# A mixture-of-experts block: first-layer weights loaded 2 MB at a time, 16 KB per partition, into places for pairs of slots

## The chip, the cores and the metric

The kernel runs on one core of a Trainium2 chip. The metric is the device time of one execution in microseconds (us); the time before is the median of three runs. All arithmetic on the path is float32 or float32 split into two parts; the output must agree with the reference.

## The reference

One decoder block on 256 tokens of 1024 channels, cut to what matters here (adaLN vectors `sh`, `sc`, `ga` come from the conditioning vector `c`):

```python
h = rmsnorm(x, g_mix) * (1 + sc1) + sh1
p = h @ w_in                                   # 1024 -> 8192
merged = sigmoid(p[GC]) * conformer_conv(p[CA], p[CB]) + sigmoid(p[GH]) * hgrn2(p[Q], p[F], p[I], p[G])
x = x + ga1 * (merged @ w_out)
h2 = rmsnorm(x, g_ffn) * (1 + sc2) + sh2
# mixture of experts: 32 experts, the best 4 for each token
u = h2[tokens of e] @ w1[e] + b1[e]            # 1024 -> 2048
y = clamped_swiglu(u) @ w2[e] + b2[e]          # 1024 -> 1024
x = x + ga2 * (sum of y over a token's experts, weighted)
return rmsnorm(x, g_final)
```

Each expert has 8 MB of `w1` and 4 MB of `w2` (MB here is 1024 KB), so the 32 experts bring 384 MB to the core, each byte once.

## The kernel before, in words

The program has two stages. The **mix stage** computes everything up to the router: the adaLN vectors, the product with `w_in` in blocks of 256 columns (each loaded, split in a high and a low part by ACT and by DVE or POOL, and multiplied on PE), the convolution on DVE, the recurrence, and the products with `w_ho`, `w_co` and `w_wo`. Then the **expert loop** takes experts e = 0 to 31 in order. For each it has 64 places for tokens; `gather` (line 953) picks the tokens' columns from `x2` by a matmul with a 0/1 matrix `o`, the first layer (lines 1000 and 1007) multiplies with eight row blocks `kt` of `w1`, activation and a transpose follow, and the second layer (line 1046) multiplies with four chunks of `w2`. Results are added back to the tokens two experts at a time. From e = 3 on an expert with more than 64 tokens has a second, smaller pass behind a branch (lines 1089 to 1127 and 1143 to 1157); in this input one expert takes it, e = 25. For that pass the loop holds an expert's weights until its first or second layer is over; for e = 0 to 2 every block is released as soon as it is used.

**Loads.** All weights pass through one list, `pending`, in one order, and SP's queue issues them in it (line 126). A load needs a free place; SP waits in order, so a load that waits for its place holds back all behind it. There are eight completion counters, so a load also waits until the one eight places ahead of it has landed. Before, the places are one pool, `big`, of 22 slots of 8 KB per partition, for loads and for working tiles alike. In the mix stage the table `LOADS` says after which release how many loads are issued; in the expert loop every release (`free`) issues as many as there is room for (`pump`). `w1` comes as eight loads of 1 MB (`kt`: 128 rows, one row of 8 KB per partition), `w2` as four of 1 MB (two rows of 4 KB, side by side, per partition). The tile `x2` keeps one slot in the expert loop, 21 are left for weights, which is 12 for one expert and 9 for the next.

PE and SP keep the program's order in the expert loop. In the rows of the order below, `w_w_1_3` of 128x2048 is a 1 MB load, of 128x4096 a 2 MB load; the name has the expert and the piece, and `w1` and `w2` share the name: the order in the list tells them apart.

Of the kernel before, what the change touches and what calls it, by code (L numbers as in the profile page):

```python
# [17 lines left out]
P = 128  # L18
# [15 lines left out]
NSLOT = 22  # L34
# [7 lines left out]
LOADS = (19, 0, 0, 0, 0, 0, 1, 0, 0, 1, 0, 0, 0, 0, 1, 2, 2, 2, 2, 0, 0, 1, 0, 0, 1, 1, 0, 0, 1, 0, 0, 1, 1, 0, 0, 1, 0, 0, 0, 0, 0, 0, 0, 0, 0, 1, 0, 0, 0, 1, 1, 0, 0, 0, 0, 0, 0, 1, 1, 0, 0, 1, 1, 0, 0, 1, 0, 0, 0, 0, 0, 0, 1, 0, 0, 1, 1, 0, 0, 1, 0, 0, 0, 0, 0, 1, 0, 0, 1, 1, 0, 0, 1, 1, 2, 0, 0, 0, 0, 3, 1, 0, 0, 1, 1, 0, 0, 1, 1, 3, 0, 0, 0, 0, 0, 0, 0, 0, 0, 1, 1, 1, 0, 1, 1, 2, 0, 0, 1, 0, 0, 1, 0, 0, 1, 0, 0, 1, 1, 0, 0, 0, 0, 0, 1, 1, 0, 0, 0, 0, 1, 1, 2, 1, 0, 0, 1, 0, 0, 1, 0)  # L42
# [48 lines left out]
def block_kernel(ctx, tc, xT_d, x_d, prm_d, con_d, wada0_d, wada_d, bada_d, gfin_d, win_d, wco_d, who_d, wo_d,  # L91
# [28 lines left out]
    def load():  # L120
# [3 lines left out]
        t = into if into is not None else slot(shape, "w_" + "_".join(map(str, key)), parts[0][1].dtype)  # L124
# [135 lines left out]
    ss = column_total(column_parts(xsq, "ss"), "ss")  # L260
    free()
# [20 lines left out]
    hx = [split_slot(f"h{i}") for i in range(2)]  # L282

    def mod_first(kt):
# [6 lines left out]
        free()  # L291
# [72 lines left out]
    def split_half(n, i):  # L364
# [4 lines left out]
        if i == 0:  # L369
            parts[key] = [fetch(key)]  # L370
# [1100 lines left out]
```

## Time and profile before

| | us |
|---|---|
| median of 3 runs (1325.0 to 1326.93) | 1326.85 |
| the profiled execution's own time | 1329.73 |
| its span in the trace | 1328.1 |
| PE busy | 1219.3 (92%) |
| DMA moved | 480 MB, 361 GB/s over the span |
| expert loop, first matmul of e = 0 to the end | 393.35 to 1328.1 |

PE is TensorE's matmul stream, PEld its weight loads, DVE VectorE, ACT ScalarE, POOL GpSimd, SP the engine that issues the loads. DMA share is the mean busy share of the 16 DMA engines, and packets are what one engine moves at a time. In the profile's own counts MB and GB are powers of ten: a load of 1024 KB is 1.049 MB there. The profiled execution is 2.9 us slower than the median, and sums on its trace are differences that apply to both.

### The profile page before, as it was taken

What the parts mean: (1) busy time and instruction counts of PE and PEld (TensorE: products, weight loads), DVE (VectorE), ACT (ScalarE), POOL (GpSimd) and SP (SyncE); (2) the same over time, 40 slices, a digit from 0 to 9 for tenths busy, and PEclk for the clock granted to TensorE, in tenths of its full rate; (3) what the DMA queues carried; (4) which work ended last, traced back from release to release, by engine and by line L of the source; (5) the groups of instructions that cost most, each with busy time, mean ns of one, the idle gap of its engine ahead of it and who ended that gap; (6) DMA issues with size and microseconds to landing.
All of it is one profiled execution on the core that took longest, in us unless ns stands there. A gap on an engine that the chain in (4) does not pass through costs nothing. (4 is left out here: it accounts for less than half of the span.)

```text
span 1328.1 us, 18971 instructions
## 1 busy us (share of the span) xinstructions
PE 1219.3 (92%) x7725; PEld 658.5 (50%) x7725; DVE 562.7 (42%) x1148; ACT 276.3 (21%) x439; POOL 146.3 (11%) x64
## 2 busy tenths in 40 slices
PE   5999999999899999999998998988888988999997
PEld 3899777679874443443333443333333332434432
DVE  4498999644853333332332233132322232323322
ACT  4445434654340001000010010001000000100112
POOL 3257435213300000000000000000000000000000
PEclk9999989999999999999999999999999999999999
DMA  9993336637669999999999999999999999999995
GB/s 381 409 401 119 138 128 220 222 105 291 252 271 393 421 421 419 421 420 420 421 419 421 420 420 420 421 421 419 420 420 419 419 420 420 421 409 420 420 419 213
DMA packets 71398, 480.01 MB, mean 361 GB/s; under 512 B 7521, under 2 KB 8801, under 8 KB 15970
## 3 DMA queue, kind: packets, MB, share of 16 engines
q1 hardware_dynamic: 70834, 477.47, 88.1%
q8 instruction: 91, 1.49, 0.5%
q10 hardware_dynamic: 432, 0.72, 0.2%
q14 instruction: 41, 0.34, 0.1%
HBM read 477.11 MB, written 1.05 MB: 360 GB/s over the span
## 5 line engine op out<-in xcount | busy, mean ns | idle before, releaser
L1007 PE MATMUL u_gl<-w_w,xg 128*64 128x512 f32 x1024 | 274.6, 599 | 27.8 <-DMA w_w<-in_w_dram 26.5
L1007 PE MATMUL u_lin<-w_w,xg 128*64 128x512 f32 x1024 | 271.7, 594 | 0.0
L1046 PE MATMUL yp<-w_w,li 128*64 128x512 f32 x992 | 223.0, 599 | 11.9 <-ACT li L1033 10.5
L1014 DVE TENSOR_SCALAR gl<-u_gl 128x512 f32<-128x512 f32 (+1 forms) x33 | 22.3, 675 | 334.7 <-PE u_gl L1007 326.4
L1007 PEld LDWEIGHTS u_gl<-w_w,xg 128*64 128x64 f32 x1024 | 76.6, 137 | 171.7 <-issue 87.7
L1007 PEld LDWEIGHTS u_lin<-w_w,xg 128*64 128x64 f32 x1024 | 81.5, 137 | 140.0 <-issue 140.0
L390 PEld LDWEIGHTS p_ps<-h,ws 128*128 128x128 f32 x1152 | 140.2, 192 | 12.5 <-issue 6.7
L390 PE MATMUL p_ps<-h,ws 128*128 128x256 f32 x1152 | 145.2, 286 | 0.0
L1046 PEld LDWEIGHTS yp<-w_w,li 128*64 128x64 f32 x992 | 69.4, 138 | 147.4 <-issue 125.3
L1056 DVE TENSOR_TENSOR yg<-yp,ga 64x512 f32<-64x512 f32 x60 | 41.3, 688 | 215.4 <-PE yp L1046 214.7
L376 POOL TENSOR_TENSOR ws<-w_in,ws 128x1024 fp32r<-128x1024 f32 x45 | 113.5, 2538 | 122.2 <-ACT ws L374 113.9
L1015 ACT ACTIVATE u_gl<-gl 128x512 f32<-128x512 f32 (+1 forms) x33 | 19.4, 589 | 430.2 <-DVE gl L1014 430.2
L1264 POOL PARTITION_BROADCAST w_gfin<-w_gfin x1 | 1.3, 1302 | 898.1 <-DMA w_w<-in_w_dram 898.1
L441 DVE SCALAR_TENSOR_TENSOR cv<-u,pre,cv 128x255 f32<-128x255 f32 (+25 forms) x240 | 95.2, 460 | 9.1 <-ACT cv L438 8.3
L953 PE MATMUL xg_ps<-o,w_x 128*128 128x128 f32 (+1 forms) x512 | 62.9, 282 | 14.1 <-DVE li L1016 10.2
L374 ACT CAST ws<-w_in 128x1024 fp32r<-128x1024 f32 x64 | 66.0, 1046 | 46.6 <-PE p_ps L390 23.6
L953 PEld LDWEIGHTS xg_ps<-o,w_x 128*128 128x128 f32 x512 | 60.1, 196 | 26.9 <-DVE li L1016 21.7
L1059 ACT ACTIVATE ys0h<-yg,by 64x512 fp32r<-64x512 f32 x30 | 21.6, 720 | 242.6 <-DVE yg L1056 242.6
L957 DVE TENSOR_SCALAR xg<-xg_ps,g,sh 128x128 f32<-128x128 f32 (+1 forms) x128 | 43.1, 401 | 18.2 <-issue 9.4
L1033 ACT COPY li<-ta 128x512 f32<-128x512 f32 (+1 forms) x33 | 18.9, 572 | 118.8 <-PE ta L1031 110.9
L376 DVE TENSOR_TENSOR ws<-w_in,ws 128x1024 fp32r<-128x1024 f32 x19 | 25.0, 1333 | 14.1 <-ACT ws L374 14.1
L390 PE MATMUL wo_ps<-ws,mg 128*128 128x256 f32 x192 | 26.2, 297 | 3.5 <-ACT ws L374 1.8
(298 smaller groups left out, 1149.0 us busy)
## 6 DMA issues: line engine op xcount, KB each, us to landing
w_w<-in_w_dram SPq DMA_DIRECT2D x380, 1024.0 KB, 19.8
w_in<-in_win_dram SPq DMA_DIRECT2D x32, 1024.0 KB, 11.0
w_ada<-in_wada_dram SPq DMA_DIRECT2D x24, 1024.0 KB, 15.9
w_ho<-in_who_dram SPq DMA_DIRECT2D x4, 1024.0 KB, 4.7
w_co<-in_wco_dram SPq DMA_DIRECT2D x4, 1024.0 KB, 5.0
w_wo<-in_wo_dram SPq DMA_DIRECT2D x4, 1024.0 KB, 9.6
w_w<-in_w_dram SPq DMA_DIRECT2D x8, 512.0 KB, 15.2
xT<-in_xT_dram SPq DMA_DIRECT2D x1, 1024.0 KB, 7.1
```

Of the source, the lines that this page charges most:

```text
L374: nc.scalar.copy(out=to[:, 0], in_=w[:, ks, :])
L376: (nc.vector if dve else nc.gpsimd).tensor_tensor(out=to[:, 1], in0=w[:, ks, :], in1=to[:, 0].bitcast(F32), op=ALU.subtract)
L390: nc.tensor.matmul(out, lhsT=lt, rhs=rh, start=first and kt == 0 and i == 0, stop=kt == KT - 1 and i == 2, skip_group_check=not first)
L441: nc.vector.scalar_tensor_tensor(out=cv[:, ct, s:], in0=u[i][:, m, :T - s], scalar=tap, in1=cv[:, ct, s:], op0=ALU.mult, op1=ALU.add)
L953: nc.tensor.matmul(ps[:, i, cs], lhsT=x2[:, t, kt * P:(kt + 1) * P], rhs=o[:, 0, t, cs], start=t == 0, stop=t == NT - 1)
L957: nc.vector.tensor_scalar(out=xg[h][:, i, cs], in0=ps[:, i, cs], scalar1=g2[:, kt:kt + 1], scalar2=sh2[:, kt:kt + 1], op0=ALU.mult, op1=AL ...
L1007: nc.tensor.matmul(up[nb][g * 64:(g + 1) * 64, :], lhsT=xg[kt // 4][:, kt % 4, i * CAP:(i + 1) * CAP], rhs=w[:, c:c + 512], start=False, s ...
L1014: nc.vector.tensor_scalar(out=gl[:, c], in0=up[0][:, c], scalar1=LIMIT, scalar2=None, op0=ALU.min)
L1015: nc.scalar.activation(si[:, c], gl[:, c], AF.Sigmoid, scale=ALPHA)
L1046: nc.tensor.matmul(yp[g * 64:(g + 1) * 64, :], lhsT=aT[:, kt % 4, kt // 4, :], rhs=w[:, kk, g * 512:(g + 1) * 512], start=False, stop=kt = ...
L1056: nc.vector.tensor_tensor(out=y[rows, :], in0=yp[gs, :], in1=ga2[gs, :], op=ALU.mult)
L1059: nc.scalar.activation(hi[rows, :], y[rows, :], AF.Copy, scale=by[rows, :])
```

## The change

`w1` is loaded as four pieces of 256 rows. Partition p holds the two neighbouring rows 2p and 2p+1 of the piece, 16 KB in one run. So the rows of `w1` that a matmul multiplies are 0, 2, 4, ... or 1, 3, 5, ... of a piece, and the token columns are picked in the same order: `gather` takes every second column of `x2` (`pick_columns`), and the scale and shift of the norm are turned once into that order (`turn_scale`, four small DMAs on ACT's queue into `by_rows`). For e = 0 the tokens were picked by `gather_rows` (matmuls of 512 columns, then four transposes); now `gather(o, half=0)` does it, 32 records of 64 columns.

The pool of 22 slots becomes 8 single slots (`big`) and 7 pairs (`two`). `w1` and most working tiles live in pairs, and `w2`, `x2` and the `w_in` blocks in singles. A piece of `w1` gives its pair back whole. The table `LOADS` is gone: after every release `pump` issues the head of the list as long as `room` finds a place of its kind; `spare` and `most_w1` limit it in the mix stage. For e = 1 the list is reordered so that the last piece of `w1` comes after the first two chunks of `w2`.

```diff
-NSLOT = 22
+NSLOT = 8
+NPAIR = 7
...
-LOADS = (19, 0, 0, 0, 0, 0, 1, 0, 0, 1, 0, 0, 0, 0, 1, 2, 2, 2, 2, 0, 0, 1, 0, 0, 1, 1, 0, 0, 1, 0, 0, 1, 1, 0, 0, 1, 0, 0, 0, 0, 0, 0, 0, 0, 0, 0, 1, 0, 0, 0, 1, 1, 0, 0, 0, 0, 0, 0, 1, 1, 0, 0, 1, 1, 0, 0, 1, 0, 0, 0, 0, 0, 0, 0, 1, 0, 0, 1, 1, 0, 0, 1, 0, 0, 0, 0, 0, 1, 0, 0, 1, 1, 0, 0, 1, 1, 2, 0, 0, 0, 0, 3, 1, 0, 0, 1, 1, 0, 0, 1, 1, 3, 0, 0, 0, 0, 0, 0, 0, 0, 0, 0, 1, 1, 1, 0, 1, 1, 2, 0, 0, 1, 0, 0, 1, 0, 0, 1, 0, 0, 1, 1, 0, 0, 0, 0, 0, 1, 1, 0, 0, 0, 0, 1, 1, 2, 1, 0, 0, 1, 0, 0, 1, 0)
...
+    two = ctx.enter_context(tc.tile_pool(name="two", bufs=NPAIR))
...
+    def pair(name, dt=F32, shape=(2 * D,)):
+
+        pairs[0] += 1
+        assert pairs[0] <= NPAIR, name
+        t = two.tile([P, 2] + list(shape), dt, tag="d", name=name)
+        return t, [t[:, i] for i in range(2)]
...
+        if key[0] == "w1":
+            pairs_w1[0] += 1
+            whole, t = pair(nm)
+            nc.sync.dma_start(out=whole.rearrange("p k f -> p (k f)"), in_=src)
+            loaded[key] = t
+            return
...
+    def room():
+        key, _, _, into = pending[0]
+        if key[0] == "w1":
+            return pairs_w1[0] < most_w1 and pairs[0] < NPAIR
+        if key[0] == "ada0":
+            return key[1] % 2 or pairs[0] < NPAIR
+        return into is not None or live[0] < NSLOT - spare
+
     def pump():
 
-        if spare is None:
-            for _ in range(next(plan, 0)):
-                load()
-        else:
-            while pending and live[0] < NSLOT - spare:
-                load()
+        while pending and room():
+            load()
...
+    def free_pair(n=1, w1=0):
+        pairs[0] -= n + w1
+        pairs_w1[0] -= w1
+        pump()
...
-        for kt in range(KT):
-            queue(("w1", e, kt), [P, 2 * FF], w1_d[e, kt * P:(kt + 1) * P, :])
+        first = len(pending)
+        for c in range(KT // 2):
+            queue(("w1", e, c), None, w1_d[e, c * 2 * P:(c + 1) * 2 * P, :].rearrange("(p k) f -> p (k f)", k=2))
...
+        if e == 1:
+
+            pending[first + 3:first + 6] = pending[first + 4:first + 6] + pending[first + 3:first + 4]
...
+    def turn_scale():
+        for h in range(2):
+            for k in range(2):
+                nc.scalar.dma_start(out=by_rows[h * 64:(h + 1) * 64, :, k::2], in_=scale2[k::2, :, h::2])
...
-                    nc.tensor.matmul(ps[:, i, cs], lhsT=x2[:, t, kt * P:(kt + 1) * P], rhs=o[:, 0, t, cs],
+                    nc.tensor.matmul(ps[:, i, cs], lhsT=pick_columns(x2[:, t, :], kt), rhs=o[:, 0, t, cs],
                                      start=t == 0, stop=t == NT - 1)
...
-    spare = 0
+    pump()
...
-    xg = gather_rows(o)
+    xg = gather(o, half=0)
...
-            return keep(w1h, ("w1", e, kt)) if inline else take(("w1", e, kt))
+            if kt % 2 == 0:
+                keep(w1h, ("w1", e, kt // 2))
+            elif not inline:
+                free_pair(0, 1)
+            return w1h[kt // 2][kt % 2]
...
-            free(KT)
+            free_pair(0, KT // 2)
```

On SP's queue, before, these are the loads that stand around the start of the expert loop: the end of e = 1 (first row the last block of its `w1`, then its four chunks of `w2`) and the beginning of e = 2. The names in brackets are what a load waits for: DMAHW is the counter of the load eight places ahead, the others are the engine that last used the place.

```order
L126 DMA w_w_1_7_4262<-in_w_dram 128x2048 [waits DMAHW7_49,PE_49]
L126 DMA w_w_1_0_4264<-in_w_dram 128x2048 [waits DMAHW0_49]
L126 DMA w_w_1_1_4266<-in_w_dram 128x2048 [waits DMAHW1_49,PE_49]
L126 DMA w_w_1_2_4272<-in_w_dram 128x2048 [waits DMAHW2_49,PE_49]
L126 DMA w_w_1_3_4278<-in_w_dram 128x2048 [waits DMAHW3_49,PE_49]
L126 DMA w_w_2_0_4284<-in_w_dram 128x2048 [waits DMAHW4_49,PE_49]
L126 DMA w_w_2_1_4290<-in_w_dram 128x2048 [waits DMAHW5_49,PE_49]
```

From the second chunk of `w2` of e = 1 on, each load waits for PE to have used one more block of e = 0. The same place of SP's queue in the changed kernel, from the third piece of `w1` of e = 1 (128x4096 is a piece of `w1`, 128x2048 a chunk of `w2`):

```order
L140 DMA w_w_1_2_4090<-in_w_dram 128x4096 [waits DMAHW4_49,DVE_49,Pool_49]
L140 DMA w_w_1_3_4210<-in_w_dram 128x4096 [waits DMAHW5_49,PE_49]
L153 DMA w_w_1_2_4212<-in_w_dram 128x2048 [waits DMAHW6_49]
L153 DMA w_w_1_3_4293<-in_w_dram 128x2048 [waits DMAHW7_49,PE_49]
L140 DMA w_w_2_0_4295<-in_w_dram 128x4096 [waits DMAHW0_49]
L140 DMA w_w_2_1_4297<-in_w_dram 128x4096 [waits DMAHW1_49]
L140 DMA w_w_2_2_4299<-in_w_dram 128x4096 [waits DMAHW2_49]
L140 DMA w_w_2_3_4348<-in_w_dram 128x4096 [waits DMAHW3_49,PE_49]
```

The fourth chunk of `w2` of e = 1 takes the eighth single, which is the place of the first chunk of `w2` of e = 0; three pieces of `w1` of e = 2, whose pairs wait for nothing more, stand behind it.

Later in SP's queue of the changed kernel, from the branch of e = 25's second pass (the row of line 1345 is the branch behind the first layer, that of line 1379 the branch behind the second):

```order
L1345 COMPARE_AND_BRANCH
L1345 UNCONDITIONAL_BRANCH x2
L140 DMA w_w_26_3_10793<-in_w_dram 128x4096 [waits DMAHW3_49,PE_49]
L153 DMA w_w_26_0_10795<-in_w_dram 128x2048 [waits DMAHW4_49]
L153 DMA w_w_26_1_10797<-in_w_dram 128x2048 [waits DMAHW5_49]
L153 DMA w_w_26_2_10799<-in_w_dram 128x2048 [waits DMAHW6_49]
L1379 COMPARE_AND_BRANCH
L1379 UNCONDITIONAL_BRANCH x2
L153 DMA w_w_26_3_10896<-in_w_dram 128x2048 [waits DMAHW7_49,PE_49]
L140 DMA w_w_27_0_10898<-in_w_dram 128x4096 [waits DMAHW0_49]
```

The last piece of an expert's `w1` waits for the first layer of the expert before, and the last chunk of its `w2` for the second layer of the expert before.

On PE, before, the start of e = 0's tokens stood as 8 rows of line 967, 4 transposes of line 973, and lines 1000 and 1007; in the changed kernel PE's queue there reads (line 1052 is the first layer, old line 1007):

```order
L1016 MATMUL xg_ps<-o,w_x 128x64
L984 LDWEIGHTS one_107
L984 MATMUL pc<-rt,one_107 128x32
L985 LDWEIGHTS one_107
L985 MATMUL pc<-rt,one_107 128x32
L1016 MATMUL xg_ps<-o,w_x 128x64 x15
L1045 LDWEIGHTS hots
L1045 MATMUL u_gl<-b_3513,hots 64x512
```

A gather of 64-column records stands where the products of 512 columns and the transposes stood.

## Rows read from the trace of the kernel before

**Rows 1.** The page, parts 1 and 2: busy time and share of PE and DVE, and for 40 equal slices of 33.2 us the busy tenths of PE and of the DMA engines, and GB/s.

```profile
PE 1219.3 (92%) x7725; PEld 658.5 (50%) x7725; DVE 562.7 (42%) x1148; ACT 276.3 (21%) x439; POOL 146.3 (11%) x64
...
PE   5999999999899999999998998988888988999997
...
DMA  9993336637669999999999999999999999999995
GB/s 381 409 401 119 138 128 220 222 105 291 252 271 393 421 421 419 421 420 420 421 419 421 420 420 420 421 421 419 420 420 419 419 420 420 421 409 420 420 419 213
```

**Rows 2.** The table by stages: stretch, its length, then for PE, PEld, DVE, ACT and POOL the busy us and the count, PE's granted clock, the DMA engines' busy share and GB/s.

```profile
33.20:100.00 66.80, 66.25 (x564) 60.49 (x557) 44.62 (x100) 28.84 (x42) 28.84 (x12) 0.99 0.99 403
100.00:233.00 133.00, 124.86 (x1727) 108.84 (x1725) 124.86 (x237) 59.88 (x98) 71.11 (x29) 0.96 0.42 152
233.00:393.40 160.40, 152.28 (x1105) 130.23 (x1105) 95.42 (x138) 78.60 (x127) 34.92 (x14) 0.97 0.61 232
...
393.40:416.10 22.70, 22.36 (x120) 10.37 (x120) 7.29 (x21) 1.19 (x2) 0.00 (x0) 1.00 0.87 349
...
440.80:700.00 259.20, 247.12 (x1210) 102.63 (x1208) 81.62 (x184) 25.07 (x38) 0.00 (x0) 0.99 1.01 420
700.00:1125.80 425.80, 376.72 (x1804) 148.01 (x1804) 123.91 (x281) 36.90 (x57) 0.00 (x0) 0.99 1.01 420
1125.80:1306.90 181.10, 172.48 (x899) 71.68 (x897) 52.06 (x116) 20.69 (x37) 1.30 (x1) 0.99 1.01 415
```

**Rows 3.** What PE's weight loads waited for (us in total, times, longest): the first row of the stretch 700 to 1130, then one row of the stretch 1160 to 1328.

```profile
PEld u_gl L1007 <- DMA w_w<-in_w_dram: 74.6, 58, 2.4
...
PEld u_gl L1007 <- DMA w_w<-in_w_dram: 2.5, 9, 0.3
```

**Rows 4.** PE's rows in order of time (start us, us, engine, line, operation, out<-in, count, idle before it): the first product of `gather_rows`; the start of e = 0's first layer, its gather and second layer; the end of e = 25's first layer and its second pass; the starts of e = 26 and e = 31; the end of e = 31's first layer.

```profile
388.50 1.04 PE L967 MATMUL rows_ps<-w_x,o 128*64 128x512 f32 x2 [0.17 <-DVE o L905]
...
393.35 1.08 PE L1007 MATMUL u_gl<-w_w,xg 128*64 128x512 f32 x4
...
406.28 1.03 PE L1007 MATMUL u_lin<-w_w,xg 128*64 128x512 f32 x4
...
409.05 3.68 PE L953 MATMUL xg_ps<-o,w_x 128*128 128x64 f32 x32
...
414.11 7.09 PE L1046 MATMUL yp<-w_w,li 128*64 128x512 f32 x32 [0.34 <-ACT li L1033]
...
1124.73 1.03 PE L1007 MATMUL u_lin<-w_w,xg 128*64 128x512 f32 x4
1125.69 1.07 PE L1089 MATMUL arm_ps<-w_x,owt 128*32 128x512 f32 x8
...
1157.20 1.99 PE L1157 MATMUL acc<-arm,owt 64*128 64x512 f32 x8 [0.83 <-DVE arm L1153]
...
1159.58 0.60 PE L1007 MATMUL u_gl<-w_w,xg 128*64 128x512 f32 x2
...
1290.93 1.05 PE L1007 MATMUL u_gl<-w_w,xg 128*64 128x512 f32 x4
...
1306.85 1.98 PE L1067 MATMUL acc<-ys,owt 64*128 64x512 f32 x4
```

**Rows 5.** SP's waits from 393 to 440 (us in total, times, longest), SP's single load at 416.09 and at 426.83 in order of time, and, for the loads at 395.3, 426.83 and 1102.96 alone, the time from issue to landing (min/median/max of one).

```profile
SPq L126 <- PE u_lin L1007: 30.5, 16, 10.4
SPq L126 <- PE yp L1046: 12.3, 4, 8.3
...
416.09 0.33 SPq L126 DMA_DIRECT2D w_w<-in_w_dram  x1
...
426.83 0.33 SPq L126 DMA_DIRECT2D w_w<-in_w_dram  x1
...
DMA to landing us min/median/max: 5.1/5.1/5.1
...
DMA to landing us min/median/max: 11.5/11.5/11.5
...
DMA to landing us min/median/max: 20.8/20.8/20.8
```

**Rows 6.** The DMA queues: packets, MB, share of 16 engines. First from 393.7 to 438.3; then from 700 to 900 (loads of 8 KB rows, with the count of packets under 512 B, which are the completion counts); then from 1304.1 to 1312.9 (loads of 2 KB rows).

```profile
q1 hardware_dynamic: 2239, 16.38, 91.0%
...
DMA packets 11526, 84.05 MB, mean 420 GB/s; under 512 B 1282, under 2 KB 1282, under 8 KB 1282
q1 hardware_dynamic: 11507, 83.77, 100.8%
q8 instruction: 15, 0.25, 0.5%
...
DMA packets 1316, 2.55 MB, mean 289 GB/s; under 512 B 80, under 2 KB 80, under 8 KB 1315
q1 hardware_dynamic: 1315, 2.53, 75.9%
```

**Rows 7.** The same view from 54.9 to 95.4, where loads of 4 KB rows and of 8 KB rows alternate.

```profile
DMA packets 3076, 16.80 MB, mean 415 GB/s; under 512 B 258, under 2 KB 258, under 8 KB 1798
q1 hardware_dynamic: 3071, 16.74, 101.2%
```

More of the change, by code (lines that the diff above doesn't have):

```diff
@@ L102, in block_kernel @@
     live = [0]
+    pairs = [0]
     pending = []
     loaded = {}
-    plan = iter(LOADS)
-    spare = None
+    spare = 1
+    pairs_w1 = [0]
+    most_w1 = 0
     def slot(shape, name, dt=F32):
@@ L123, in load @@
         parts = src if isinstance(src, list) else [(None, src)]
-        t = into if into is not None else slot(shape, "w_" + "_".join(map(str, key)), parts[0][1].dtype)
+        nm = "w_" + "_".join(map(str, key))
+        if key[0] == "w1":
[5 more added lines that the diff above has]
+        if key[0] == "ada0":
+            if key[1] % 2 == 0:
+                halves[:] = pair(nm)[1]
+            t = halves[key[1] % 2].rearrange("p (k n) -> p k n", k=KT)
+        elif into is not None:
+            t = into
+        else:
+            t = slot(shape, nm, parts[0][1].dtype)
         for at, part in parts:
@@ L281, in block_kernel @@
     s1 = of_pre(KT)
-    hx = [split_slot(f"h{i}") for i in range(2)]
+    hx = split_pair("h")
     def mod_first(kt):
@@ L290, in mod_first @@
                                  start=i == 0, stop=i == 1)
-        free()
+        if kt % 2:
+            free_pair()
         sb = temp("mod0s")
@@ L369, in split_half @@
         if i == 0:
-            parts[key] = [fetch(key)]
+            parts[key] = [fetch(key)] + split_pair("ws")
         w = parts[key][0]
-        to = split_slot("ws")
+        to = parts[key][1 + i]
         ks = slice(i * 4, i * 4 + 4)
@@ L377, in split_half @@
                                                         op=ALU.subtract)
-        parts[key].append(to)
         if i == 1:
@@ L393, in split_y @@
     def split_y(i):
[L394 removed]
+        if i == 0:
+            yx.extend(split_pair("y"))
         for kt in range(i * 4, i * 4 + 4):
@@ L411, in block_product @@
                     prod_kt(ps[:, m, :], kt, w, a, full if tokens_out else ms, ms if tokens_out else full, tokens_out, m == 0)
-            free(2 if last else 1)
+            if i == 1:
+                free_pair(2 if last else 1)
             if middle and i == 0:
@@ L600, in hgrn_out @@
         square_sums(*before)
-        free(3)
+        free_pair()
         orr = temp("orr")
@@ L617, in hgrn_out @@
                 yield
-        free(1)
+        free_pair()
     rbs = fix.tile([P, E], F32, name="rbs")
@@ L678, in block_kernel @@
         parts.pop(units[n])
-        free(2)
+        free_pair()
+    spare = 2
     free()
+    cv = slot([P, KT, T], "cv")
+    spare = 1
     order.__exit__(None, None, None)
@@ L702, in block_kernel @@
             if q is None:
-                q = slot([P, HEADS, T], "q")
+                q, k = (x.rearrange("p (h t) -> p h t", h=HEADS) for x in pair("qk")[1])
             nc.scalar.activation(q[:, cs, :], ps, AF.Copy, scale=float(P) ** -0.5)
@@ L732, in block_kernel @@
                 step(lv1, 100)
-                free(3)
+                free_pair()
+                free()
                 norms.append(hgrn_out())
         else:
-            if gates[i // 2] is None:
-                gates[i // 2] = slot([P, 2, KT // 2, T], "gates")
+            if gates[0] is None:
+                gates = pair("gates", F32, (2, KT // 2, T))[1]
             nc.scalar.activation(gates[i // 2][:, part - 6, i % 2 * 2:i % 2 * 2 + 2, :], ps, AF.Sigmoid)
@@ L766, in block_kernel @@
     split_y(1)
+    most_w1 = 2
     free()
@@ L781, in block_kernel @@
         nc.vector.tensor_tensor(out=lo, in0=tm, in1=hi.bitcast(F32), op=ALU.subtract)
-        if b % 2 == 1:
-            free()
+        if b == 3:
+            most_w1 = 4
+            free_pair()
         step(preps, 2)
@@ L840, in block_kernel @@
             prod_kt(ps[:, t, :], kt, w, mg, slice(0, 256), slice(t * P, (t + 1) * P), True)
-    free(4)
+    most_w1 = NPAIR
+    free_pair(2)
     residual(ps, 3, 1)
@@ L956, in gather @@
                 kt = h * 4 + i
[L957 to L976 removed]
+                nc.vector.tensor_scalar(out=xg[h][:, i, cs], in0=ps[:, i, cs], scalar1=by_rows[:, 0, kt:kt + 1],
+                                        scalar2=by_rows[:, 1, kt:kt + 1], op0=ALU.mult, op1=ALU.add)
         return xg
```

64 lines of the change are left out of this document (25 added, 39 removed).

## The prediction

> **What bounds the kernel now.** I began with the page's first parts: PE is busy for 92% of the span, but from about 395 us the DMA engines are at 9 tenths and 420 GB/s in nearly every slice [rows 1]. Two resources are near full, so I read them by stage. Up to 393.4 PE stands idle for only 0.6 + 8.1 + 8.1 = 16.8 us after the first 33 us, and DVE is busy for 124.86 of 133 us in the middle, while the loads run at 152 to 232 GB/s: the mix stage is not bound by loads [rows 2]. In the expert loop the busy share of DMA is 1.01 from 440.8 to 1125.8, and PE's falls from 247.1 of 259.2 to 376.7 of 425.8 [rows 2]. The waits say why: from 700 to 1130 PE's weight loads wait 74.6 us for loads, in 58 places, and after 1160 only 2.5 us [rows 3]. An expert's 12 loads are 12.58 MB (1.049 MB each), at 420 GB/s 29.96 us. PE without such waits needs (1290.93 − 1159.58)/5 = 26.3 us, from the start of e = 26 to that of e = 31 [rows 4]. So PE uses up its reserve, then follows the loads, until e = 25, whose second pass holds PE from 1125.69 to 1159.58 and gives the loads their lead back [rows 4]. From 1125.7 to the end PE sets the time; before that, from about e = 13, the loads do. Whatever delays the stream of loads up to the last `w1` row of e = 25 delays the end by as much; whatever shortens it is gained up to there.
>
> **The start of the loop: a gap in the loads.** Before, all 21 places are filled when e = 0 starts: 12 loads of e = 0, eight `w1` and one `w2` of e = 1. The last chunk of `w2` of e = 2, load 36, is issued at 426.83 and lands 11.5 later, at 438.3 [rows 5]. From 393.7 to there the queue moves 16.38 MB, some 15.6 loads at 369 GB/s, so it idles a little there too [rows 6].
>
> In the changed kernel the order of SP's queue sets other waits. Seven singles hold `w2`: four chunks of e = 0 and three of e = 1. The third piece of `w1` of e = 1 is in, so 20 MB have landed. The last piece waits until PE has used two row blocks: eight take 407.31 − 393.35 = 13.96, one 1.74, so 393.35 + 3.5 and 0.2 to issue = 397.1 [rows 4]. A load on an idle queue lands 5.1 after its issue [rows 5], the second MB 2.5 later (1.049/0.420): 404.7; the third chunk of `w2` 407.2. The fourth chunk takes the place of the first chunk of `w2` of e = 0, which PE uses only in its second layer, from 414.11 [rows 4]. Before, SP issued a load into that very release at 416.09 [rows 5]; the same wait now has the three pieces of e = 2 behind it, whose pairs are free. So it lands at 416.09 + 5.1 = 421.2, and the queue idles for 421.2 − 2.5 − 407.2 = 11.5 us. Then come eight MB of `w1` and four of `w2`: 12 × 2.485 − 0.33 (below) = 29.5, to 450.7 instead of 438.3. **Cost: 12.4 us of lost lead.** PE itself feels nothing at once: it needs the first of them more than 25 us later. The bounds: 9 (if the piece before lands late, the gap shrinks) and 14.
>
> **The longer rows: the gain.** From 700 to 900 the queue used 100.8% of 16 engines for 11507 − 1282 = 10225 packets of 8 KB: 3225.6/10225 = 0.3155 us each. From 1304.1 to 1312.9, with rows of 2 KB, 0.759 × 16 × 8.8/(1315 − 80) = 0.0865 us [rows 6]. The difference is 6 KB, so 2 KB cost 0.0763 and 0.0102 us is fixed in each packet. A packet of 16 KB then takes 0.6208 in place of 0.6310. A load of 1 MB has four such packets on each engine, so 0.041 us, and eight MB save **0.33 us per expert**. From e = 3 to 25 that is 23 × 0.33 = **7.6 us**. The lower bound is 0 (a row that is moved as two packets of 8 KB). The upper one comes from rows of 4 KB beside rows of 8 KB: 1.012 × 16 × 40.5 = 655.8 us, less 1273 packets of 0.3155, leaves 254.2 for 1540 packets of 4 KB, 0.165 each, so the fixed part is 0.0147 [rows 7], 0.47 per expert, 10.8 us. I take the value from the rows farthest apart, 7.6.
>
> The Trainium skill ("DMA: Bandwidth & Descriptors", "Why small descriptors are slow") puts the fixed part at some 3 cycles per packet beside 32 bytes a cycle, and calls it a matter of small descriptors. An estimate by that page is 1.5 cycles saved of 259, 0.6%, or 2.7 us in place of 7.6, and the sum would end at 1338.6. The measured step from 2 KB to 8 KB rows speaks for more than that [rows 6].
>
> **The larger piece.** PE may start a block when its load has landed. Before, one block (1.74) follows the last landing, now two: **+1.7 us**, at the end of e = 25's first layer, nowhere else on the path.
>
> **The first gather.** Before, line 967 starts at 388.50 and the first layer at 393.35; now 32 records, like those of e = 0's other half (3.68 us) [rows 4], end at 392.2, and with scaling, and 0.5 for the two products ahead, the first layer starts at 393.2 to 394.1. I take +0.3. The later gathers read every second column; they lie where PE waits for loads anyway up to e = 25. All later times hang on this start, the gap too, since a PE event ends it.
>
> **The mix stage.** PE's order there is the same; loads come earlier or later by the greedy rule, at half of the DMA rate, beside a full DVE. I take 0: the cover is DVE's 124.86 of 133. Bounds: −16.8, all of PE's idle time [rows 2], and +5.1, one load that PE waits for from its issue [rows 5]; near 0 because no stretch there has the DMA engines above 0.61. The four small DMAs on ACT come long before their first reader.
>
> **The sum.** +12.4 − 7.6 + 1.7 + 0.3 = **+6.8 us**. The load issued at 1102.96 landed at 1123.8 before the change; now the last piece lands at about 1128.9 and the layer ends near 1132.5 instead of 1125.7. The 202 us behind stay. The profiled execution becomes 1329.73 + 6.8 = 1336.5; it lies 2.9 above the median, and on the median's scale it is 1326.85 + 6.8 = **1333.7**.
>
> What is late next: with seven singles the last `w2` chunk of e = 26 waits for the end of e = 25's second pass, now 1159.1 + 6.8 = 1165.9, so it lands at 1171.0, some 3 us after its turn (1128.9 + 16 × 2.485 − 0.3 = 1168.4). The last `w1` of e = 31 comes 72 loads behind that of e = 25 (179 us): 1128.9 + 179 + 3 − 2 = 1308.9, and two blocks later 1312.4; PE arrives at 1306.85 + 6.8 = 1313.7. So PE still ends last, by about 1 us, and a smaller packet gain would make this second route the longer.
>
> **The rivals.**
> *No gain from the rows.* If 16 KB are moved at the price of two 8 KB packets, the sum is 12.4 + 1.7 + 0.3 = 14.4: 1341.3. For it: the rate is already 419 to 421 GB/s at 8 KB [rows 1]. Against it: the step from 2 KB to 8 KB [rows 6].
> *The gap is paid back: no change.* The packets save 0.51 to 0.74 per expert, so 11.7 to 17 us: about 1327. The rows of 4 KB reach 0.47, just short [rows 7]. The Trainium skill (same page, "Where 436 GB/s comes from") names a ceiling of 435.2 GB/s; rows that ran at it would take 2.409 per load and save 0.61 per expert, 14.0, which ends at 1327.2; no slice of this trace is above 421 [rows 1].
> *Faster: the loop begins earlier.* The table of loads is replaced by a rule that issues as soon as a place is free. If splits and casts got their blocks earlier, PE could regain part of its 16.8 idle us [rows 2]; it decides from 9.5 us on (6.8 + 2.7), and with 12.8 of them gone the time is 1320.9. Against it: DVE is nearly full in the middle stretch, and pairs give places back later than singles.
> *16 KB packets are slow.* The queue of instruction fetches moves packets of 16 KB (0.25 MB in 15), 0.5% of 16 × 200 us: 1.07 us each [rows 6]. At that price a `w1` of 32 packets per engine would cost 32 × 0.45 = 14 us more, 430 us over 30 experts. It is another queue, with another target, and a lone packet.
>
> **How the numbers follow.** The forecast, 0.59, own range 1330.0 to 1338.5 (gains of 10.8 to 2.7). No gain 0.16. Paid back 0.12. Earlier start 0.11. Slow packets 0.02. About 0.2%, 2.7 us, can be told from no change; the forecast's lower edge gives a little of its chance to no change, the start of the loop may help there too: faster 0.12, same 0.13, slower 0.75. The range of 1326.0 to 1341.5 leaves out the slow packets, the earlier start and half of the largest losses.
>
> **What will show it.** Right: a DMA trough of some 11.5 us at 407 to 419, SP waiting for line 1091 (the second layer) over it; packets of 16 KB near 0.62 us and 423 to 425 GB/s in the loop; PE's waits for loads beginning earlier than before, by e = 9 to 12; e = 25's first layer ending 6 to 8 us later; from there the same 202 us. Wrong: a start of the loop off 393.4 by more than 2 us; no trough; 420 GB/s as before; the end of the loop later against e = 25 than before, which would mean that the loads bind again at e = 31.

## The result and the profile after

The changed kernel took 1341.55 us (median of 6 runs, 1333.92 to 1343.02) beside 1326.70 for the kernel before, timed with it. The ratio is 1.0105, 95% interval 1.0089 to 1.0122: 13.9 us slower (11.8 to 16.2); the two medians lie 14.8 apart. The forecast was +6.8 and a range up to 1341.5. The profiled execution took 1340.79, its span is 1339.0.

The first parts of the page after, in the same form as [rows 1], and the row of the queue that carries the loads:

```profile
PE 1219.6 (91%) x7745; PEld 670.0 (50%) x7745; DVE 567.9 (42%) x1147; ACT 272.9 (20%) x438; POOL 149.2 (11%) x64
...
PE   6999799999899999999799988988888998899998
...
DMA  9865544459666999999999999999999999999995
GB/s 382 331 221 217 190 147 170 169 181 354 245 267 276 428 423 423 425 424 425 426 424 425 424 423 425 424 425 424 425 425 422 421 425 425 390 383 425 425 425 227
...
q1 hardware_dynamic: 52402, 477.46, 86.8%
```

PE is as busy as before. The loads run at 423 to 426 GB/s in the loop instead of 419 to 421, so the longer rows are faster. What is lost stands ahead of slice 14: 331 and 221 in the second and third slice where 409 and 401 stood, and 276 in the thirteenth where 393 stood. The table by stages, cut where PE's rows put the same events as in [rows 2] (the last column is GB/s, the one before it DMA's share, the one before that PE's granted clock):

```profile
33.20:100.00 66.80, 65.79 (x568) 59.89 (x568) 53.95 (x116) 32.45 (x48) 31.70 (x13) 1.00 0.76 278
100.00:233.00 133.00, 123.41 (x1717) 109.43 (x1716) 120.30 (x222) 54.33 (x91) 67.24 (x28) 0.95 0.51 183
...
396.00:418.90 22.90, 22.56 (x120) 10.48 (x118) 6.42 (x18) 1.19 (x2) 0.00 (x0) 1.00 0.47 185
418.90:443.30 24.40, 24.23 (x132) 10.91 (x128) 9.86 (x24) 2.52 (x4) 0.00 (x0) 1.00 0.95 402
443.30:700.00 256.70, 236.44 (x1144) 100.17 (x1146) 77.53 (x173) 23.75 (x37) 0.00 (x0) 0.99 1.01 425
700.00:1136.30 436.30, 386.56 (x1870) 155.20 (x1870) 129.29 (x293) 38.30 (x59) 0.00 (x0) 0.99 1.01 424
```

Where [rows 2] had a DMA share of 0.87 (393.4 to 416.1), it is now 0.47 (396.0 to 418.9). That is the trough. SP's waits from 396 to 440, its rows in order of time, and the time to landing of the two loads issued at 399.61 and at 418.85, to be read beside [rows 5]:

```profile
SPq L153 <- PE yp L1091: 18.4, 1, 18.4
...
399.61 0.33 SPq L140 DMA_DIRECT2D w_w<-in_w_dram  x1
399.99 19.18 SPq L153 DMA_DIRECT2D w_w<-in_w_dram  x2
419.23 8.96 SPq L140 DMA_DIRECT2D w_w<-in_w_dram  x4
...
w_w<-in_w_dram SPq DMA_DIRECT2D x1, 2048.0 KB, 8.6
...
w_w<-in_w_dram SPq DMA_DIRECT2D x1, 1024.0 KB, 4.9
```

SP waits 18.4 us for the second layer of e = 0 (line 1091), with three pieces of 2 MB behind the waiting load whose pairs are free; they follow from 419.23 on (the fourth of that row waits for PE). By their landings in the trace the chunk ahead of it was in at 411.3, the waiting one at 423.7, and it moved for 2.5 us itself: the queue stood idle for 423.7 − 2.5 − 411.3 = 9.9 us.

PE's rows in order of time, the same events as in [rows 4], with two of the new waits at e = 9:

```profile
395.97 1.03 PE L1052 MATMUL u_gl<-w_w,xg 128*64 128x512 f32 x4
...
416.87 7.09 PE L1091 MATMUL yp<-w_w,li 128*64 128x512 f32 x32 [0.34 <-ACT li L1078]
...
647.96 1.08 PE L1052 MATMUL u_gl<-w_w,xg 128*64 128x512 f32 x4 [1.24 <-DMA w_w<-in_w_dram]
...
652.87 1.08 PE L1052 MATMUL u_gl<-w_w,xg 128*64 128x512 f32 x4 [1.25 <-DMA w_w<-in_w_dram]
...
1136.25 1.06 PE L1134 MATMUL arm_ps<-w_x,owt 128*32 128x512 f32 x8
...
1169.44 1.03 PE L1052 MATMUL u_gl<-w_w,xg 128*64 128x512 f32 x4
...
1302.12 1.05 PE L1052 MATMUL u_gl<-w_w,xg 128*64 128x512 f32 x4
...
1318.04 1.98 PE L1112 MATMUL acc<-ys,owt 64*128 64x512 f32 x4
```

The layer of e = 25 ends 10.6 us later than in [rows 4] (1136.25 against 1125.69), and 2.6 of them were there at the start of the loop (395.97 against 393.35). The two waits are 4.91 apart, one per 2 MB piece: two blocks, then a wait. From 1136.25 to the end of the span it is 202.8 us (202.4 before).

### The profile page after: what moved, and what is told of

It is laid out like the page before. It is cut to its first block, busy times and chain, and to the rows that moved or that the text cites. A ratio compares the mean times of both kernels' runs of the same rounds, so it can differ in the third digit from the quotient of the medians.

```text
span 1339.0 us, 18731 instructions
## 1 busy us (share of the span) xinstructions
PE 1219.6 (91%) x7745; PEld 670.0 (50%) x7745; DVE 567.9 (42%) x1147; ACT 272.9 (20%) x438; POOL 149.2 (11%) x64
## 5 line engine op out<-in xcount | busy, mean ns | idle before, releaser
L1091 PE MATMUL yp<-w_w,li 128*64 128x512 f32 x992 | 223.8, 599 | 15.7 <-ACT li L1078 10.5
L1016 PE MATMUL xg_ps<-o,w_x 128*128 128x128 f32 (+1 forms) x544 | 71.0, 290 | 17.1 <-DVE li L1061 10.3
L1016 PEld LDWEIGHTS xg_ps<-o,w_x 128*128 128x128 f32 x544 | 67.6, 201 | 30.4 <-DVE li L1061 21.7
L428 ACT CAST ws<-w_in 128x1024 fp32r<-128x1024 f32 x64 | 64.1, 1048 | 13.9 <-DMA w_in<-in_win_dram 13.8
L1020 DVE TENSOR_SCALAR xg<-xg_ps,by_rows 128x128 f32<-128x128 f32 (+1 forms) x136 | 45.4, 396 | 24.8 <-PE xg_ps L1016 24.6
L430 DVE TENSOR_TENSOR ws<-w_in,ws 128x1024 fp32r<-128x1024 f32 x19 | 31.4, 1672 | 9.7 <-ACT ws L428 9.7
```

Of the source, the lines that this page charges most:

```text
L428: nc.scalar.copy(out=to[:, 0], in_=w[:, ks, :])
L430: (nc.vector if dve else nc.gpsimd).tensor_tensor(out=to[:, 1], in0=w[:, ks, :], in1=to[:, 0].bitcast(F32), op=ALU.subtract)
L1016: nc.tensor.matmul(ps[:, i, cs], lhsT=pick_columns(x2[:, t, :], kt), rhs=o[:, 0, t, cs], start=t == 0, stop=t == NT - 1)
L1020: nc.vector.tensor_scalar(out=xg[h][:, i, cs], in0=ps[:, i, cs], scalar1=by_rows[:, 0, kt:kt + 1], scalar2=by_rows[:, 1, kt:kt + 1], op0=A ...
L1091: nc.tensor.matmul(yp[g * 64:(g + 1) * 64, :], lhsT=aT[:, kt % 4, kt // 4, :], rhs=w[:, kk, g * 512:(g + 1) * 512], start=False, stop=kt = ...
```

## The experiments

Two theories went in. *Lead*: the loads start the loop late, because SP's order holds free pairs behind a chunk of `w2`, and nothing gives that lead back until e = 25. *Granularity*: places for pairs come free later and larger pieces make PE wait longer, so no order of loads helps. A third question came with the first result: what the mix stage costs, which the prediction had put at 0.

**The kernel before, once more (e0_before).**

> The kernel before, unchanged, for a second profile of it. Both theories: 1324 to 1331; the start of the expert loop within 1 us of 393.4 if the mix stage is steady; if it wanders by 2 us or more, part of the changed kernel's later start (396.0) is no property of it.

It took 1326.0, near its median, and its first layer of e = 0 starts at 390.79 instead of 393.35. So the profile the prediction used started its loop 2.6 us later than a run that is nearer to the median. Other kernels with the mix stage of before start at 389.8 and 391.7 (below). Differences of less than 2.6 us at the start, read from one profile each, mean nothing. Some profiled executions also lie above the median of their kernel: by 2.4 us in e1, 3.2 in e3 and 4.0 in e10.

**The list in the order of releases (e1_release_order).** Edit to the changed kernel, up to e = 5: each piece or chunk stands in the list where its place comes free.

```diff
+    for e in range(6):
+        early += [("w1", e + 1, 3)] * (e > 0) + [("w1", e + 2, c) for c in range(3)]
+        early += [("w2", e + 1, 3)] + [("w2", e + 2, c) for c in range(3)]
```

> The changed kernel, with the list of loads in the order in which places come free up to e = 5: after the first layer of e the last piece of w1 of e + 1 and three pieces of e + 2, after its second layer the last chunk of w2 of e + 1 and three of e + 2. Lead theory (the loads lose their lead because a load at the head of the list waits for a place of the other kind): the trough behind e = 0 goes, and so do the smaller waits up to e = 5; e = 25's first layer ends 11 to 12 us earlier than in the changed kernel (1124 to 1125 in place of 1136.3), and the time is about 1330, ratio to before 1.000 to 1.004. Rival (the lead is not what decides; the rows bring nothing, or the mix stage is what got longer): the trough goes, but the time stays within 3 us of the changed kernel's 1341.5, ratio 1.008 to 1.012.

Measured: 1329.78, ratio 1.0024 (1.0009 to 1.0038). The stages of this kernel from the start of its loop:

```profile
394.20:416.00 21.80, 21.80 (x107) 9.89 (x104) 4.66 (x13) 0.60 (x1) 0.00 (x0) 0.91 0.76 308
416.00:440.00 24.00, 23.66 (x120) 9.09 (x119) 8.32 (x21) 2.63 (x4) 0.00 (x0) 1.00 1.01 426
```

With the trough gone, at the same pieces of 2 MB, e = 25's first layer ends 730.8 us after the start of the loop (740.3 in the changed kernel, 732.3 before). Granularity falls as the main cause; lead stands. The time is still 3 us above before, although this stretch is shorter. In its profile the loop starts 0.9 us later, and what follows e = 25's first layer takes 205.5 us instead of 202.4, 2.1 of it in the second pass (36.0 us at a granted clock of 0.91; before, 33.9 at 0.95).

**The same for one expert alone (e2_one_gap).**

```diff
-    for e in range(6):
+    for e in range(1):
```

> The changed kernel, with one step of the list moved: three pieces of w1 of e = 2 come before the last chunk of w2 of e = 1. The trough of 10 to 11.5 us at e = 0 goes. If the trough itself is the cost, the time falls by 10 to 11 us, to about 1331. If the lead is bounded by the places as a whole (what is loaded earlier fills them, and the next load of the other kind waits in its turn), some 8 us of idle come back at the last chunk of w2 of e = 2, and the time falls only by 3 to 4 us, to 1338. Rival without lead: no change, 1341.5.

Measured: 1337.72, ratio 1.0081 (1.0059 to 1.0103), 3.8 less than the changed kernel. From 420 to 445 the DMA share of this kernel is 0.70: the idle time comes back one expert later, behind the last chunk of `w2` of e = 2. So it is not one slip in the list: the next last chunk waits in the same way, and with the same places only the order of e1, kept up to e = 5, takes the idle time away.

**Rows of 8 KB in pieces of 2 MB (e3_rows_8k).** The list, the places and the size of a load are those of the changed kernel; the rows are the old ones, and the turned scale is gone.

```diff
-            nc.sync.dma_start(out=whole.rearrange("p k f -> p (k f)"), in_=src)
+            nc.sync.dma_start(out=whole, in_=src)
...
-... w1_d[e, c * 2 * P:(c + 1) * 2 * P, :].rearrange("(p k) f -> p (k f)", k=2))
+... w1_d[e, c * 2 * P:(c + 1) * 2 * P, :].rearrange("(k p) f -> p k f", k=2))
```

> The changed kernel with loads of 2 MB as they are, but two rows 128 apart in each partition, 8 KB each, and the token columns picked without a stride; order, places and pieces stay. If rows of 16 KB save 0.32 us per expert, the loads take 2.485 per MB again and the end comes 7 to 8 us later than in the changed kernel, 1349, ratio to before 1.015 to 1.018. If they save nothing that reaches the end, or are paid for by the stride of the picked columns, the time stays at 1341.5, ratio 1.009 to 1.012.

Measured: 1346.19, ratio 1.0147 (1.0123 to 1.0171), a little under what was expected. The queue from 700 to 900, first in the changed kernel, then in this one (packets, MB, GB/s; then packets, MB, share of 16 engines):

```profile
DMA packets 7828, 84.86 MB, mean 424 GB/s; under 512 B 867, under 2 KB 867, under 8 KB 867
...
q1 hardware_dynamic: 7809, 84.59, 100.4%
```

```profile
DMA packets 11104, 84.08 MB, mean 420 GB/s; under 512 B 855, under 2 KB 855, under 8 KB 855
...
q1 hardware_dynamic: 11086, 83.82, 100.9%
```

The second has the rate of [rows 6] again, so the 1% belongs to the rows of 16 KB and not to the size of the load. Counted from each loop's start, e = 25's first layer ends 747.2 − 740.3 = 6.9 us later without them, 0.30 per expert over 23.

**Fewer places in the kernel before, two tries (e5_before_less, e7_before_hold).** If lost lead costs what it delays, then four slots less up to e = 11 must hurt the kernel before too.

```diff
-        spare = 3 if e == RELOAD_AFTER else 0
+        spare = 3 if e == RELOAD_AFTER else 4 if e < 12 else 0
```

> The kernel before, with four of its 22 slots kept empty in the expert loop up to e = 11, then all in use again. No load is larger or in another order. If lost lead is paid one for one, four loads of 2.485 us less in store make e = 25's first layer end 9.9 us later (about 1133 to 1136), and the time is 1336, ratio 1.0065 to 1.0085. If lead is made good later by the loads (the rival to the lead theory), the time stays within 3 us of before, ratio under 1.0023.

Measured: 1325.70, ratio 0.9996 (0.9983 to 1.0009), a miss, and no test: the DMA share from 416 to 440 is 0.98, so the loads had lost nothing. A limit on what the program counts only moved the instructions that issue; the places were there. In e7_before_hold four slots are therefore taken by tiles that small DMAs read at e = 31 (extra work of no use to the output):

```diff
+        if len(idle_places) < 4:
+            live[0] -= 1
+            idle_places.append(slot([P, 2048], f"idle{len(idle_places)}"))
```

> The kernel before, with four of its 22 slots taken out of use for good: the first four that e = 0's first layer releases get a tile that is held to the end. (The run before this one kept four free only in the program's count; the loads still got their places in time, so no load waited longer.) Lead theory: the loads wait at e = 0 until its fifth block is used, then for its second layer, and at e = 3 once more; some 8 to 11 us of idle at the start of the loop, e = 25's first layer ends 8 to 11 us later than 1122 to 1126, and the time is 1334 to 1337, ratio 1.006 to 1.0085. If lead is made good later (rival), under 1.0023.

Measured: 1338.71, ratio 1.0096 (1.0080 to 1.0112). The same event as in [rows 4], after the last block of e = 25:

```profile
1134.30 1.06 PE L1089 MATMUL arm_ps<-w_x,owt 128*32 128x512 f32 x8
```

It comes 742.6 after that loop's start (391.68), 10.3 later than before. Its 80th load of expert weights lands 165.6 after the start, before 155.7, so 9.9 of lead were lost: lead is worth its full length up to e = 25 in 1 MB loads as well, with nothing of the change in the kernel. The time is above what was expected because the loads bind once more at e = 31.

**One chunk earlier still (e6_release_early, e8_early_8k).** The list of e1_release_order, and the third chunk of `w2` of e = 1 ahead of that expert's `w1`; e8_early_8k is this with rows of 8 KB, as in e3_rows_8k.

```diff
+    early.remove(("w2", 1, 2))
+    early.insert(early.index(("w1", 1, 0)), ("w2", 1, 2))
```

> The list of loads of the release-order run, and besides the third chunk of w2 of e = 1 ahead of that expert's w1, into a single that is empty while pairs are still waited for at the end of the mix stage. Lead theory: it lands in idle time of the queue, the lead at the start of the loop grows by one load of 2.5 us, and the time falls by 2 to 3 us against the release-order run, to about 1327, ratio to before 0.999 to 1.002. Rival (the start of the loop is set by the pairs that come late, and what is loaded before them only moves the rest back): no change against the release-order run, 1329 to 1331, ratio 1.002 to 1.004.

Measured: 1326.68, ratio 1.0002 (0.9988 to 1.0015).

> The list of loads of the run before last (release order, one chunk of w2 early), with rows of 8 KB as in the third run (two rows 128 apart in each partition, loads still of 2 MB). If rows of 16 KB save 0.30 us per expert on the loads wherever the loads set the pace, this is 6 to 8 us slower than with 16 KB: 1333 to 1335, ratio to before 1.005 to 1.007. If that run's gain came from the order alone, it stays at 1326.7, ratio 0.999 to 1.0015.

Measured: 1335.47, ratio 1.0067 (1.0047 to 1.0087). The pair confirms the sign of the rows' gain, but 8.8 us is more than it can be. Between the two profiles 5.0 us are there before the loop begins (395.27 against 390.28) and 4.3 in it, fewer than the rows should bring: from 440 to 700 e6's loads run at 418 GB/s, where e1's run at 424, and e8's at 420. And up to e = 25 e6's loop is no shorter than e1's (730.6 against 730.8); what e6 won is that its loop started 3.9 us earlier. The rows of 150 to 190 us, first of the changed kernel, then of e6, show where:

```profile
150.00:190.00 40.00, 34.39 (x507) 30.50 (x506) 40.00 (x74) 12.92 (x22) 15.25 (x6) 0.83 0.42 149
```

```profile
150.00:190.00 40.00, 34.40 (x596) 31.81 (x595) 40.00 (x74) 16.04 (x26) 17.29 (x7) 0.91 0.44 147
```

PE is busy for as long, but at a granted clock of 0.83 in the changed kernel (in e1 and e8 as well) and of 0.91 in e6: 40 × 0.08 is 3.2 us of full clock. So the start of the loop, put at +0.3, moves by as much as the rows bring, and here most of it is the clock.

**The mix stage.** This is how it looks in the changed kernel. ACT's wait for the blocks of `w_in` from 30 to 390 (us, times, longest; before there is no such wait); then POOL's and DVE's rows at the splits that follow (start, us); then PE's rows behind them:

```profile
ACT ws L428 <- DMA w_in<-in_win_dram: 13.8, 4, 6.8
...
161.49 8.12 POOL L430 TENSOR_TENSOR ws<-w_in,ws 128x1024 fp32r<-128x1024 f32 x3 [0.79 <-ACT ws L428]
...
158.55 2.70 DVE L536 TENSOR_TENSOR qk<-qk,f 128x512 f32<-128x512 f32 x1
161.17 0.68 DVE L537 TENSOR_TENSOR qk<-qk,f 128x512 f32<-128x512 f32 x1
...
162.12 2.51 DVE L536 TENSOR_TENSOR qk<-qk,f 128x512 f32<-128x512 f32 x1
164.54 2.83 DVE L537 TENSOR_TENSOR qk<-qk,f 128x512 f32<-128x512 f32 x1
...
167.52 1.08 PE L522 MATMUL lv<-qk 128*32 128x32 f32 x64 [5.07 <-DVE qk L537]
168.53 8.06 PE L443 MATMUL p_ps<-ws,h 128*128 128x256 f32 x48
...
166.00:178.00 12.00, 10.48 (x193) 10.20 (x194) 12.00 (x24) 1.37 (x2) 3.60 (x2) 0.72 0.47 176
```

An operation that takes DVE 0.68 us takes 2.5 to 2.8 while POOL splits beside it. Here five splits follow one another, probably because their blocks came late (no run changed that alone); before, four stood apart, and from 140 to 240 PE's longest wait for DVE was 2.0 us. PE waits 5.07 us for the last of the slow operations, and the 48 products behind it take 8.06 where 6.01 is usual, at a granted clock that falls to the lower of its two levels (1.2 of 2.4 GHz) for part of the stretch, 0.72 on the mean. The Trainium skill ("SBUF — State Buffer", "SBUF: two separate sides") has VectorE and GpSimd share one pair of ports as an exclusive lock in which the loser waits for the whole instruction; these rows agree: DVE's operations are longer by 1.8 to 2.2 us beside splits of 2.7 us (8.12 for three).

Four kernels tried to move it. e9_mix_spare is e6 with one place more for `w_in` blocks up to block 8.

```diff
-    spare = 1
+    spare = 0
...
+        if n == 8:
+            spare = 1
```

> The run with release order and the early chunk of w2, and besides one more single for loads in the first part of the mix stage (none is kept spare until the ninth block of w_in, where one is kept again for the tile f). In the changed kernel ACT's casts waited 13.8 us for w_in loads, 12.3 of it at 114 to 129 us; before, not at all. Theory (the mix stage starts the loop some 2 to 3 us later because w_in blocks come late into few singles, so that POOL's splits fall beside DVE's chain of the recurrence): the early loads come up to 10 us sooner, the casts wait less than 8 us, and the loop starts 0 to 3 us earlier; time 1324 to 1327, ratio 0.998 to 1.0005. Rival (the casts' wait is idle time of ACT that costs nothing, and the start is set by DVE's own work): start and time as in that run, ratio 0.9995 to 1.0015.

Measured: 1330.08, ratio 1.0030 (1.0019 to 1.0042). Both expectations missed. ACT's wait for `w_in` stayed at 12.7 us in 3 times, so the edit did not take away what it was to take away; the loop started at 397.19, with a granted clock of 0.83 from 150 to 190 and 0.96 up to 330. Why the one place costs this was not found.

e10_split_half and e11_split_dve are e6 with the splits of two of those blocks moved from POOL to DVE, half of each or all.

```diff
-SPLIT_HALF = (4, 6, 17, 19, 21, ...
+SPLIT_HALF = (4, 6, 17, 18, 19, 20, 21, ...
```

> The list of loads of e6_release_early; the second halves of the splits of blocks 18 and 20 go from POOL to DVE. They are two of the five POOL splits that lie between 155 and 170 us, where DVE's rows of 128x512 took 2.5 to 2.8 us instead of 0.68 and PE then waited 5.1 us for them. Theory (the mix stage's loss is POOL's splits beside DVE's recurrence): POOL's block there shrinks from 5 splits to 3, PE's wait for qk falls from 5.1 to about 3, the loop starts some 2 us earlier than in a kernel with five, and the time is 1324 to 1326, ratio 0.9985 to 1.0. Rival (the start of the loop wanders with PE's granted clock, and DVE is full there whatever POOL does): wait for qk 5 to 6.5 us, ratio 1.0 to 1.0015.

Measured: 1329.79, ratio 1.0025 (1.0014 to 1.0036). The wait shrank to 2.9 as the theory had it, but the time grew as neither had it; its loop started at 398.93. PE's idle time from 100 us to the start is that of e6 (19.2 against 19.3 us), but between the same times PE was at the lower clock for 33.5 us, in e6 for 14.6.

```diff
-SPLIT_DVE = (3, 4, 6, 28, ...
+SPLIT_DVE = (3, 4, 6, 18, 20, 28, ...
```

> As e10_split_half, but blocks 18 and 20 are split by DVE alone, so that one POOL split is left between 155 and 170 us (four splits of 128x1024 more on DVE, 1.21 us each, 4.8 us). Theory (POOL's splits slow DVE's recurrence): the 128x512 rows of DVE there are back at 0.68, PE's longest wait for qk is under 2 us, the loop starts 3 to 4 us earlier than with five, and the time is 1322.5 to 1325.5, ratio 0.997 to 0.9995. Rival (DVE is full there, so 4.8 us of work more on it come on top): PE's waits for DVE grow by 2 to 5 us, ratio 1.001 to 1.004.

Measured: 1323.29, ratio 0.9984 (0.9974 to 0.9993): the one version ahead of both kernels, by 2.1 us. Its rows of POOL, DVE and PE in the same stretch:

```profile
160.86 7.08 POOL L443 TENSOR_TENSOR ws<-w_in,ws 128x1024 fp32r<-128x1024 f32 x1 [23.38 <-PE p_ps L456]
...
164.39 0.68 DVE L549 TENSOR_TENSOR qk<-qk,f 128x512 f32<-128x512 f32 x1
164.99 0.68 DVE L550 TENSOR_TENSOR qk<-qk,f 128x512 f32<-128x512 f32 x1
...
169.23 0.75 PE L535 MATMUL lv<-qk 128*32 128x32 f32 x64 [0.77 <-DVE qk L550]
```

DVE is back at 0.68 nearly throughout, the one POOL split takes 7.08 instead of 2.4 (now POOL is the one that waits), and PE's wait has shrunk to 0.77. The time and the wait came as the theory had it; the start of the loop did not: 390.42, the same as e6's 390.28. PE was 6.1 us ahead of e6 at the next block and lost that again: from 190 to 233 it is busy for 38.27 us where e6 has 40.47, and from 233 to 330 its granted clock is 0.96 where e6 has 1.00. What e11 won against e6 therefore stands behind the start, up to e = 25's first layer (727.8 against 730.6 us): 1.2 of it is in e = 0's first block, which e6 ran at the lower clock, and the rest was not followed up.

e12_before_split makes the same move in the kernel before.

> The kernel before, with nothing changed but that blocks 18 and 20 of w_in are split by DVE alone, as in e11_split_dve. Theory (the move mends what the changed kernel's late w_in loads brought, five POOL splits in a row beside DVE's recurrence): before, POOL's splits stand apart there and PE waited only 0.4 and 2.8 us, so the start of the loop moves by -1 to +2 us and the ratio is 0.999 to 1.0015. Rival (the move helps any kernel): loop start 2 to 4 us earlier, ratio 0.997 to 0.9985, and then e11_split_dve owes nothing to the pieces of 2 MB.

Measured: 1332.70, ratio 1.0046 (1.0030 to 1.0062): a miss of both; the loop started at 397.14. PE's row that shows a part of it:

```profile
233.82 1.06 PE L247 MATMUL mup<-cv,pre 128*32 128x256 f32 x2 [5.81 <-DVE cv L441]
```

Before, that wait was 0.6. DVE, with 4.8 us of splits more, is late with the convolution. PE was also at the lower clock for 30.7 us between 100 us and the start, before for 20.5 and 17.1 in two profiles. So the same move gained in one kernel and lost in the other; that it depends on which of DVE's two duties is late just then fits the rows, but was not tested.

## Why the prediction was wrong in size

The time came out at the upper edge of the range, beside the rival without a gain from the rows (1341.3). That nearness is chance: the rows did gain, and the loss came from elsewhere. The profiled execution grew by 1340.79 − 1329.73 = 11.1 us. By the prediction's steps, each read from the trace:

| step | forecast | measured |
|---|---|---|
| first gather and mix stage, to the start of the loop | +0.3 | +2.6 |
| lead lost at the start of the loop | +12.4 | +13.7 |
| longer rows, e = 3 to 25 | −7.6 | −7.5 |
| larger piece after the last landing | +1.7 | +1.7 |
| everything after e = 25's first layer | 0 | +0.4 |
| sum | +6.8 | +10.9 |

**The step that failed is "The mix stage. ... I take 0".** The rest of the difference is there too. The profile before was an execution 2.9 us above its median, with a late start. Against the second profile (390.79, 1326.0) the start is 5.2 us later, the loop 8.4 longer up to e = 25, what follows 1.2, together 14.8, which is the difference of the medians. So the loop starts 2.6 to 5.2 us late. Over all profiles, 394.0 is the mean start of the changed kernel and its five variants up to e8 (390.3 to 396.0), 391.4 that of four profiles with the old mix stage (389.8 to 393.4): the groups overlap, so the size stays uncertain. The bound that the prediction kept beside its 0, +5.1, was close to what came.

What the late start consists of can be read from PE's rows and the records of its clock between 100 us and the start. PE stands idle for 19.2 us there, before for 16.2 and 15.7 in the two profiles; in the six profiles above it is 16.9 to 19.3, in the four 15.5 to 16.2. And PE is at the lower clock for 23.9 us, before for 20.5 and 17.1, which costs half of that. Idle time thus adds 3.0 to 3.5 us, the clock 1.7 to 3.4, and about 2 come back because PE's own work is shorter. Over the 14 profiles of this case the start of the loop goes with the time at the lower clock (correlation 0.95, 0.46 us for each us), from 14.6 us in e6 to 33.5 in e10. That is why e6, with the same wait of 5.07 us, starts at 390.3. What sets how long the clock stays down was not tested.

Its reason for 0 ("no stretch there has the DMA engines above 0.61") asked whether the DMA engines had room, and not when a place came free: the greedy rule brings `w_in` later at some blocks (278 instead of 403 GB/s from 33 to 100), and DVE was full, as it was seen to be. The wait of 5.1 us and the stretched operations are in every changed kernel with five splits, and moving splits shortens the wait; both are shown. That the late blocks cause them is argued from the order of the rows only, since e9, which was to bring the blocks earlier, did not.

**The lead: right in kind, 1.3 short.** It is counted from each loop's start to the landing of load 36, or its counterpart: 454.6 − 395.97 = 58.6 against 438.3 − 393.35 = 44.9. Counted from the start, the steps came as forecast: the last piece of `w1` of e = 1 was issued 3.6 us after it (forecast 3.8), and the late chunk landed 27.8 after it (forecast 27.9). The trough was 9.9 us, not 11.5, but its length is not in the sum. The prediction had 20 MB in by the start of e = 0; the third piece of `w1` of e = 1 landed at 400.5, 4.5 us after it, so the chunk ahead of the trough came later and the trough was shorter. The 1.3 us are behind it: one load landed 3.8 us after the one ahead of it instead of 2.5 (447.2 against 443.3). e1, e2 and e7 show that lost lead costs its length.

**The rows: right.** The last `w1` of e = 25 landed at 1132.6 against 1123.8, 8.8 later, after 16.3 at load 36: 7.5 were regained, 0.32 per expert; e3 gives 0.30. Packets: 7809 − 867 = 6942 moved 84.59 MB, so 3384 of them are of 16 KB and 3558 of 8 KB; 1.004 × 16 × 200 = 3212.8 us, less 3558 × 0.3155, is 0.618 us for one of 16 KB (forecast 0.6208). The rival without a gain falls with e3, and the Trainium skill's fixed part ("DMA: Bandwidth & Descriptors", "Why small descriptors are slow"), from which 2.7 us were estimated, is too small here: 7.5. The rival of the ceiling falls as well, at 424 to 425 GB/s.

**The larger piece: right.** From the last landing to the end of the layer it was 1.98 us before and is 3.70.

**After e = 25.** The second pass waits longer once (2.0 us for DVE at its line 1144 instead of 1.2), but its whole length fell from 33.9 to 33.2, at a granted clock of 1.00 instead of 0.95. From e = 26 to e = 31 PE takes 1.3 us more (132.7 against 131.4), with no wait in its rows that was not there before; this stays open. The late chunk of e = 26 that the prediction named did not reach the end.

**What it said would show.** The trough with SP at line 1091, packets near 0.62 and 423 to 425 GB/s, PE's waits from e = 9 and the same 202 us all came. The start of the loop, 395.97, was off 393.4 by 2.6: that is the sign it had named for being wrong.

## What to carry to other kernels

Where loads bind a long stretch, the lead that they have when it begins is worth its full length: order one queue by when places come free, so that no load that waits for a late place stands ahead of loads whose places are free. Larger rows and pieces save little per load (0.3 us per 12 MB here) and split the buffers into kinds, so look first at whose place the queue's head waits for. And where an engine is full, do not price a shift in what feeds it at nothing: take the bound, or count which of its duties comes late, and read the granted clock of both kernels before a difference of a few us at one event is put down to the change.

## What the runs showed of the hardware

- DVE and POOL beside one another: 128x512 on DVE took 0.68 us alone and 2.5 to 2.8 beside POOL's splits, and one POOL split took 2.4 alone and 7.08 beside DVE's. Moving two splits from POOL to DVE went with some 2.4 us less in one kernel (e11 against e6, by their ratios) and 6.1 us more in another (e12 against before).
- Rows of 16 KB still gain over rows of 8 KB: 424 against 420 GB/s.
- Towards the end of PE's wait of 5.07 us its granted clock fell to the lower level (0.80 on the mean from 164 to 168 us, 0.50 from 168 to 172), and the same 48 products took 8.06 instead of 6.01.
- Over 14 profiles the loop started later by 0.46 us for each us that PE was at the lower clock between 100 us and the start (14.6 to 33.5 us); the extremes are e6 at 390.3 and e10 at 398.9.
